# Second part of a feed-forward block as seven block products, with the sums of its weights made in the attention stages

## The chip, the core and the metric

The kernel runs on one core of a Trainium2 chip, in one launch. The metric is the device time of that launch in microseconds (us), here the median of several runs. Five engines work side by side, each through its own list of instructions and strictly in that list's order: TensorE (PE, matrix products, with PEld for the loads of its stationary operand), VectorE (DVE), ScalarE (ACT), GpSimd (POOL) and SyncE (SP). In this kernel SP issues nearly all DMAs, so a DMA that waits on SP holds back all DMAs that stand behind it there. An instruction waits by semaphores for the data, or for the buffer, that another engine hands over. The matrix products write to PSUM, of which this stage holds eight buffers of 128x512; everything else lies in SBUF, 128 partitions wide.

## The reference

One layer of a streaming-encoder block on 1024 tokens of width 1024, in float32: a token-mixing stage with two recurrent branches and an output projection `w_out`, a cross-attention into 256 memory tokens with the weights `xa_wq`, `xa_wk`, `xa_wv`, `xa_wo`, and a gated feed-forward block with a hidden width of 2816. The change concerns the last line before the final norm:

```python
h = h + (gate_a * y_a + gate_b * y_b) @ w_out[l]
...
u = rmsnorm(h, norm_xa_g[l])
...
h = h + o @ xa_wo[l]

u = rmsnorm(h, norm_ffn_g[l])
h = h + (jax.nn.silu(u @ ffn_w1[l]) * (u @ ffn_w3[l])) @ ffn_w2[l]
return rmsnorm(h, norm_final_g)
```

## The kernel before

**Products.** Every float32 operand is split into a high part (a copy rounded to the type fp32r, made by ACT) and a low part (the operand less the high part, made by POOL or DVE). `mm3` (L297 to L301) then adds up three products: high by high (L299), high by low (L300), low by high (L301). So each block product costs three matmuls, and each operand one ACT and one POOL or DVE instruction of 128x512 (`split`, L276 to L285).

**Stages near the end.** After the mixing stage come, in this order, the keys and values of the memory, `add_project` with `w_out` over all 1024 tokens (tile `pw`, four column blocks c of 256, 8 loads of tokens `tok`), the query projection and attention, `add_project` with `xa_wo` for one half of the tokens and then for the other, the feed-forward's first part (tile `P`), and its second part (tile `acc`). In `add_project` a column block takes four weight loads of 256 KB. Its products collect in PSUM and DVE adds them to the tokens (L1724); three PSUM buffers serve them.

**First part.** For each of 11 pairs f of hidden blocks, `products` makes seven block products per weight matrix (14 with both, 12 matmuls each) and from their sums four gated blocks of hidden values, which go to the DRAM array `hid_d` as [128 hidden x 512 tokens].

**Second part.** It is computed once per half h of the tokens and per half c of the output's columns. For each of these four, 22 hidden blocks are multiplied with four token tiles: 4 x 22 x 4 x 3 = 1056 matmuls of 128x512. The hidden blocks are loaded back and split once per half (ACT L2046, POOL L2047); 14 of the 22 lie in a ring of buffers (`th`, `tl`), the other 8 in the tiles `ah`, `al`. The blocks of `w2` are loaded and split 22 times for each of the four (`operand`, ACT L281, POOL L285), with seven buffers each for the parts `wh` and `wl`. The last three hidden blocks of each of the four are worked token tile by token tile, so that the four sums end one after another (`ILAST`).

**What sets the order.** The code issues instructions per block; a scheduler with its own estimates of durations puts them in each engine's list, SP's included. So loads and splits stand earlier or later in a list than the code says; the lists are shown below where it matters.

Of the kernel before, what the change touches and what calls it, by code (L numbers as in the profile page):

```python
# [17 lines left out]
P = 128  # L18
D = 1024
# [164 lines left out]
def tile_trunk(ctx, tc, x, mem, norm_mix_g, w_in, rw_mu, rw_w0, rw_w2, rw_a0, rw_a2, rw_g2,  # L184
# [1454 lines left out]
    early_d = scratch("early_d", [2, HK, P, HALF])  # L1639
    ssq = const.tile([P, 4, 4], F32, name="ssq")  # L1640
# [5 lines left out]
    def attention_block(xctx):  # L1646
# [27 lines left out]
        Kh = kp.tile([P, KT, NM], F32R, name="Kh")  # L1674
        Kl = kp.tile([P, KT, NM], F32R, name="Kl")
        Vh = vp.tile([P, NMT, D], F32R, name="Vh")
        Vl = vp.tile([P, NMT, D], F32R, name="Vl")
# [28 lines left out]
        def add_project(a, w, src, halves, ss=None, beside=iter(())):  # L1706
# [3 lines left out]
            for c in range(D // W):  # L1710
                ww = load_w(w, c * W)
                for i2 in range(2 * halves.start, 2 * halves.stop):
# [15 lines left out]
                    if c > 1 or c == 1 and i2 % 2:  # L1728
                        next(beside, None)
# [33 lines left out]
        hs = add_project(yT, w_out, x[0], range(NHALF))  # L1763
# [79 lines left out]
        for _ in prev:  # L1843
            pass

        for h in range(NHALF):
            hs = add_project(oT, xa_wo, h1d, range(h, h + 1), *((ssq, early_blocks(hs, *fa)) if h else ()))
# [23 lines left out]
    hd = scratch("hid_d", [FT, NHALF, P, HALF])  # L1871
    def raw(src, k, c, kn, cn):
# [20 lines left out]

    def blocks():

        return [[fp.tile([P, HALF], F32, tag=t, name=f"h{t}", bufs=4 if t == "s" else 2) for t in ts] for ts in (("u2", "u3"), ("c", "s"))
                for _ in range(2)]
# [47 lines left out]
    def gated(n, C, s, f, t):  # L1945

        if n == 0:
            s = fp.tile([P, HALF], F32, tag="s", name="s", bufs=4)
            nc.scalar.activation(s, C, AF.Sigmoid)
        nc.vector.tensor_tensor(s, C, s, op=ALU.mult)  # L1950
        if n:
            nc.sync.dma_start(out=hd[f, t], in_=s)
        return s

# [17 lines left out]
    def early_products(f, T1, T4):  # L1972

        for name, T, b in (("P5", T1, "S1"), ("P4", T4, "B22")):
            for n in range(2):
                t = kept[f, name, n] = fp.tile([P, HALF], F32, tag="kept", name=name, bufs=8)
                nc.scalar.activation(t, product(name, T[n], B[b]), AF.Copy)

    def products(f, A):
# [6 lines left out]
        for n in range(2):  # L1986
# [3 lines left out]
            s = gated(n, C, s, f, 1)  # L1990
        for a11, a12, a21, a22 in A:
# [38 lines left out]
    for f in range(HF):  # L2030
        products(f, weights(f))

    fg = fp.tile([P, D], F32, name="fg", bufs=1)
    nc.sync.dma_start(out=fg, in_=norm_final_g.partition_broadcast(P))
    order = [f + e for f in range(HF) for e in (0, HF)]
    ILAST = 3
    for h in range(NHALF):
        a = act(act1)
        hid = []
        for n, f in enumerate(order):  # L2040
            if n >= FT - KT:
                hh, hl = (t[:, n - FT + KT, :] for t in a)
            else:
                hh, hl = (ring.tile([P, HALF], F32R, tag=t, name=t) for t in ("th", "tl"))
# [3 lines left out]
            hid.append((hh, hl))  # L2048
        hs = blocks()
        for i in range(4):  # L2050
            for c in range(2):
                nc.sync.dma_start(out=hs[i][c], in_=h2d[(4 * h + i) * P:(4 * h + i + 1) * P, c * HALF:(c + 1) * HALF])
        ss = sp.tile([P, 4, 8], F32, tag="ssf", name="ssf")
        for c in range(2):
            cs = slice(c * HALF, (c + 1) * HALF)
            acc = [psum("acc") for _ in range(4)]
            w2 = []
            for n, f in enumerate(order):
                w2.append(operand(raw(ffn_w2, f, c * HALF, 1, HALF), "2"))
                if n < FT - ILAST:  # L2060
                    steps = [(i, n) for i in range(4)]
                elif n == FT - 1:
                    steps = [(i, g) for i in range(4) for g in range(FT - ILAST, FT)]
                else:
                    steps = []
                for i, g in steps:
                    ts_ = slice(i * P, (i + 1) * P)
                    mm3(acc[i], hid[g][0][:, ts_], hid[g][1][:, ts_], w2[g][0][:, 0, :], w2[g][1][:, 0, :],
                        g == 0, g == FT - 1)

            sums = []

            def finish(i):

                r = ss[:, 3, i:i + 1]
                o1, o2 = hs[i]
                rows = slice((4 * h + i) * P, (4 * h + i + 1) * P)
                nc.scalar.activation(o1, o1, AF.Copy, scale=r)
                nc.sync.dma_start(out=out[rows, 0:HALF], in_=o1)
                ins = nc.vector.scalar_tensor_tensor(o2, o2, r, fg[:, HALF:D], op0=ALU.mult, op1=ALU.mult).ins  # L2080
                behind(ins, sums[-1])
                nc.sync.dma_start(out=out[rows, HALF:D], in_=o2)

            for i in range(4):
                o = hs[i][c]
                r = [ss[:, n, i:i + 1] for n in range(4)]
                sums.append(nc.vector.tensor_tensor(o, acc[i], o, op=ALU.add).ins.name)  # L2087
# [37 lines left out]
```

## Time and profile before

| | |
|---|---|
| time, median of 3 runs | 2396.96 us (2396.28 to 2398.84) |
| the profiled execution's own time | 2398.55 us |
| its span in the trace | 2396.8 us |
| PE busy | 2335.8 us, 97% |
| DVE, ACT, POOL busy | 1411.2, 1128.3, 1228.8 us |
| mean granted clock of PE | 0.993 |
| second part: first and last matmul start | 2139.3 and 2389.4 us |

A matmul's record is longer than the time from one start to the next, since matmuls overlap; what a stretch of matmuls costs is read from the starts. An instruction's idle time before it and the engine that ended it stand in brackets in the rows of the timeline.

### The profile page before, as it was taken

The page shows a single profiled execution, that of the slowest core. Times are in us where ns is not written, and L with a number is a line of the kernel's source. Part 1 is how long each engine was busy: PE and PEld are TensorE (multiplying, and loading weights), DVE is VectorE, ACT ScalarE, POOL GpSimd, SP SyncE. Part 2 cuts the span into 40 slices and gives each one's busy share as a digit, 9 for nine tenths or more (in the row PEclk, how much of TensorE's full clock was granted, in tenths as well). Part 3 has the DMA queues.
Part 4 walks back from the last instruction along what each step waited for, and adds up shares of the span by engine and source line. Part 5 has one row for each costly group of instructions (what it writes and reads, how often), then busy time and mean ns, then how long its engine had stood idle before and what let it go on. Part 6 is the DMA issues. An engine that isn't in the chain of part 4 may idle for free. (4 is left out here: it accounts for less than half of the span.)

```text
span 2396.8 us, 48780 instructions
## 1 busy us (share of the span) xinstructions
PE 2335.8 (97%) x19258; PEld 1934.3 (81%) x19258; DVE 1411.2 (59%) x2288; ACT 1128.3 (47%) x2249; POOL 1228.8 (51%) x1268
## 2 busy tenths in 40 slices
PE   7999999999999999999998999999999999999998
PEld 5777777778887878888887998889778888877887
DVE  5887874667777667767754525444687565640101
ACT  6545454646566656555663415444433333343332
POOL 3554545555466555665664511112565444477673
PEclk9999999999999999999999999999999999999999
DMA  5444445333344343434244823133723223265441
GB/s 168 122 127 121 123 117 161 74 101 85 92 109 110 82 129 105 123 89 126 56 140 152 300 69 117 53 120 132 259 80 101 84 75 93 71 199 172 158 161 57
DMA packets 386001, 288.46 MB, mean 120 GB/s; under 512 B 106171, under 2 KB 329517, under 8 KB 385773
## 3 DMA queue, kind: packets, MB, share of 16 engines
q1 hardware_dynamic: 383341, 279.58, 39.6%
q0 software_dynamic: 1344, 4.72, 0.5%
q8 instruction: 152, 2.49, 0.4%
q10 hardware_dynamic: 1088, 1.05, 0.1%
q14 instruction: 76, 0.62, 0.1%
HBM read 208.73 MB, written 76.02 MB: 119 GB/s over the span
## 5 line engine op out<-in xcount | busy, mean ns | idle before, releaser
L102 PE MATMUL pproj<-uh,whi 128*128 128x512 f32 x768 | 320.0, 417 | 1.1 <-DVE q L102 1.1
L102 PE MATMUL pproj<-uh,wlo 128*128 128x512 f32 x768 | 300.9, 392 | 2.8 <-POOL wlo L102 2.1
L102 PE MATMUL pproj<-ul,whi 128*128 128x512 f32 x768 | 301.2, 392 | 0.0
L285 POOL TENSOR_TENSOR wl<-wraw,wh 128x512 fp32r<-128x512 f32 x154 | 202.1, 1323 | 133.2 <-ACT wh L281 131.6
L285 POOL TENSOR_TENSOR wlo<-wraw,whi 128x512 fp32r<-128x512 f32 (+1 forms) x86 | 117.9, 1374 | 288.6 <-ACT whi L281 280.7
L102 POOL TENSOR_TENSOR wlo<-wraw,whi 128x512 fp32r<-128x512 f32 x96 | 129.0, 1355 | 118.8 <-ACT whi L102 103.8
L281 ACT ACTIVATE whi<-wraw 128x512 fp32r<-128x512 f32 (+1 forms) x166 | 101.0, 617 | 173.1 <-PE pw L301 62.0
L299 PE MATMUL pproj<-uh,whi 128*128 128x512 f32 (+1 forms) x432 | 179.5, 416 | 0.9 <-ACT whi L281 0.6
L281 ACT ACTIVATE wh<-wraw 128x512 fp32r<-128x512 f32 x154 | 94.3, 627 | 182.2 <-PE P L300 74.5
L301 PE MATMUL pproj<-uh,wlo 128*128 128x512 f32 (+1 forms) x432 | 171.4, 397 | 1.5 <-POOL wlo L285 1.5
L102 PEld LDWEIGHTS pproj<-uh,whi 128*128 128x128 f32 x768 | 144.4, 188 | 34.3 <-DVE q L102 2.4
L300 PE MATMUL pproj<-ul,whi 128*128 128x512 f32 (+1 forms) x432 | 170.7, 395 | 0.0
L102 PEld LDWEIGHTS pproj<-ul,whi 128*128 128x128 f32 x768 | 144.3, 188 | 32.0
L102 PEld LDWEIGHTS pproj<-uh,wlo 128*128 128x128 f32 x768 | 144.9, 189 | 28.1 <-POOL wlo L102 2.5
L285 POOL TENSOR_TENSOR wlT<-wraw,whT 128x512 fp32r<-128x512 f32 x70 | 96.6, 1386 | 96.2 <-ACT whT L281 92.5
L299 PE MATMUL pw<-whi,ah 128*128 128x256 f32 x512 | 144.6, 282 | 0.0
L300 PE MATMUL pw<-wlo,ah 128*128 128x256 f32 x512 | 144.6, 282 | 0.0
L301 PE MATMUL pw<-whi,al 128*128 128x256 f32 x512 | 144.3, 282 | 0.0
L2087 DVE TENSOR_TENSOR hu<-acc,hu 128x512 f32<-128x512 f32 x8 | 5.5, 692 | 200.0 <-PE acc L301 200.0
L285 DVE TENSOR_TENSOR wlo<-wraw,whi 128x512 fp32r<-128x512 f32 x80 | 73.7, 922 | 83.4 <-ACT whi L281 83.1
L102 ACT ACT_TABLE_LOAD x90 | 115.5, 1283 | 13.5 <-DVE m L102 6.4
L299 PEld LDWEIGHTS pproj<-uh,whi 128*128 128x128 f32 (+1 forms) x432 | 81.6, 189 | 25.4 <-issue 6.2
(457 smaller groups left out, 6656.2 us busy)
## 6 DMA issues: line engine op xcount, KB each, us to landing
wraw<-in_ffn_w_dram SPq DMA_DIRECT2D x192, 256.0 KB
wraw<-in_w_in_dram SPq DMA_DIRECT2D x148, 256.0 KB
hid_d<-s SPq DMA_DIRECT2D x44, 256.0 KB
tok<-in_x_dram SPq DMA_DIRECT2D x16, 512.0 KB
ar_d<-AR SPq DMA_DIRECT2D x32, 256.0 KB
bk_d<-BK SPq DMA_DIRECT2D x16, 512.0 KB
AR<-ar_d SPq DMA_DIRECT2D x64, 128.0 KB
BK<-bk_d SPq DMA_DIRECT2D x16, 512.0 KB
```

The lines of the kernel that those rows point to most:

```text
L102: r = getattr(self.engine, op)(*a, **kw)
L281: nc.scalar.activation(hi, src, AF.Copy)
L285: e.tensor_tensor(lo, src, hi.bitcast(F32), op=ALU.subtract)
L299: nc.tensor.matmul(ps, ah, bh, start=first, stop=False)
L300: nc.tensor.matmul(ps, ah, bl, start=False, stop=False)
L301: nc.tensor.matmul(ps, al, bh, start=False, stop=last)
L2087: sums.append(nc.vector.tensor_tensor(o, acc[i], o, op=ALU.add).ins.name)
```

## The change

The second part takes seven block products in place of eight. The hidden values X (two halves of tokens by two halves of the hidden width) and W = `w2` (two halves of the hidden width by two halves of columns) are taken as 2 x 2 blocks, and four sums of blocks of each side, with seven products of them, give the four result blocks by additions.

- **Sums of the weights** (`w2_sums`). For each of 11 pairs of row blocks: two loads of 512 KB, two DVE and two POOL subtractions of 128x512 (L1717 to L1720), and one store of 1 MB to the array `wsum_d` (L1721). Seven of the pairs are done while `add_project` works on `w_out`, in the tiles of the pool `act2`; four while it works on `xa_wo` for the first half of the tokens, in the tiles that held the keys and values.
- **Sums of the hidden values** (`hidden_sums`). For each of 11 pairs, in the first part: two DVE and two POOL instructions of 128x512 (L2010 to L2013), and four stores to `hsum_d`. One of the four stores to `hid_d` goes. The gated blocks stay in a ring of 14 buffers (`kept`) until then.
- **The second part.** 7 blocks x 11 items x 4 token tiles x 3 = 924 matmuls. Every item loads one hidden block or sum and one block of `w2` or sum (77 of each). The low part of the hidden side is made by DVE (L2200) where POOL made it; all hidden operands lie in the ring of 20. The code splits four items ahead of the product and loads eight ahead.
- **Results.** The residual tokens lie in `act1` (tile `hres`), loaded by eight DMAs of 512 KB. Products that serve several result blocks are first added up in the tiles `Uw`, `Vw` (`p1`, `p5`, `p6`, `p7`) and added to `hres` by `more` (L2149).

The diff, cut to its core:

```diff
+        def w2_sums(fs, places):
...
+            def sums(f, y):
+                y11, y12, y21, y22 = (y[:, n, :] for n in range(4))
+                nc.vector.tensor_tensor(y11, y12, y11, op=ALU.subtract)
+                nc.gpsimd.tensor_tensor(y12, y22, y12, op=ALU.subtract)
+                nc.gpsimd.tensor_tensor(y22, y22, y11, op=ALU.subtract)
+                nc.vector.tensor_tensor(y21, y22, y21, op=ALU.subtract)
+                nc.sync.dma_start(out=wsd[f], in_=y)
...
-        hs = add_project(yT, w_out, x[0], range(NHALF))
+        hs = add_project(yT, w_out, x[0], range(NHALF), every=True, beside=w2_sums(
+            w2f, [None, None] + [in_act2(tag, n) for tag in ("ah", "al", "ah") for n in range(2)] + [in_act2("al", 0)]))
...
+    def hidden_sums(f):
+        x11, x21, x12, x22 = (hid.pop(k) for k in ((f, 0), (f, 1), (f + HF, 0), (f + HF, 1)))
+        tt(x22, x21, x22, op=ALU.add)
+        nc.gpsimd.tensor_tensor(x21, x11, x21, op=ALU.subtract)
+        tt(x11, x22, x11, op=ALU.subtract)
+        nc.gpsimd.tensor_tensor(x12, x12, x11, op=ALU.subtract)
+        for n, t in enumerate((x22, x11, x21, x12)):
+            nc.sync.dma_start(out=hsd[n, f], in_=t)
...
-            nc.sync.dma_start(out=hl.bitcast(F32), in_=hd[f, h])
-            nc.scalar.activation(hh, hl.bitcast(F32), AF.Copy)
-            nc.gpsimd.tensor_tensor(hl, hl.bitcast(F32), hh.bitcast(F32), op=ALU.subtract)
...
+    ILAST, LOOK, LOADS = 3, 4, 8
+    blocks = ((lambda f: hd[f, 0], w2(0, 0), p1),
+              (lambda f: hd[f + HF, 0], w2(1, 0), lambda i, acc: add(0, i, 0, acc, ALU.add, True)),
+              (lambda f: hsd[1, f], wsum(3), p6),
+              (lambda f: hsd[0, f], wsum(0), p5),
+              (lambda f: hsd[3, f], w2(1, 1), lambda i, acc: add(0, i, 1, acc, ALU.add, False)),
+              (lambda f: hsd[2, f], wsum(1), p7),
+              (lambda f: hd[f + HF, 1], wsum(2), lambda i, acc: add(1, i, 0, acc, ALU.subtract, False)))
...
+    def split_item(b, f):
+        hl, y = loaded.pop((b, f))
+        hh = ring.tile([P, HALF], F32R, tag="th", name="th")
+        nc.scalar.activation(hh, hl.bitcast(F32), AF.Copy)
+        tt(hl, hl.bitcast(F32), hh.bitcast(F32), op=ALU.subtract)
+        ops[b, f] = (hh, hl, *operand(y, "2"))
```

What the change makes of the engines' lists is shown at three places. The first is SP's list where `add_project` starts on `w_out`; `y` are the tiles of the weight sums, `tok` the tokens. Before:

```order
L1759 DMA yraw<-y_d 128x512 x12
L1667 DMA wraw<-in_w_out_dram 128x2x256 x10
L334 DMA tok<-in_x_dram 128x1024 x8
L1667 DMA wraw<-in_w_out_dram 128x2x256 x6
L1667 DMA wraw<-in_xa_wq_dram 128x2x256 x10
L1767 DMA h_d<-tok 128x1024 x6
```

And now, from behind the first block's four weight loads, which still stand first:

```order
L1713 DMA y_16881<-in_ffn_w_dram 128x1024 x3
L334 DMA tok<-in_x_dram 128x1024 x8
L1713 DMA y_16881<-in_ffn_w_dram 128x1024
L1668 DMA wraw<-in_w_out_dram 128x2x256 x4
L1713 DMA y_17016<-in_ffn_w_dram 128x1024 x2
L1721 DMA wsum_d<-y_16881 128x2048
L1713 DMA y_17016<-in_ffn_w_dram 128x1024 x2
L1721 DMA wsum_d<-y_16881 128x2048
L1721 DMA wsum_d<-y_17016 128x2048
L1713 DMA y_17133<-in_ffn_w_dram 128x1024 x4
L1721 DMA wsum_d<-y_17016 128x2048
L1668 DMA wraw<-in_w_out_dram 128x2x256 x4
```

The second column block's four now stand behind eight 512 KB loads of tokens and four of sums; the third block's four stand behind four stores of finished sums.

The second place is DVE's list over the same stretch; `al` are low parts of the tokens' operands, `wlo` of the weights, and `tok<-pw` adds a product from PSUM to the tokens. Before:

```order
L285 TENSOR_TENSOR wlo<-wraw,whi 128x512 x2
L285 TENSOR_TENSOR al<-yraw,ah 128x512
L1702 TENSOR_TENSOR Vl<-pvv,Vh 128x2x256
L285 TENSOR_TENSOR al<-yraw,ah 128x512 x3
L285 TENSOR_TENSOR wlo<-wraw,whi 128x512
L1724 TENSOR_TENSOR tok<-pw,tok 128x256 x6
L285 TENSOR_TENSOR wlo<-wraw,whi 128x512
L1724 TENSOR_TENSOR tok<-pw,tok 128x256 x2
```

And now:

```order
L285 TENSOR_TENSOR wlo<-wraw,whi 128x512 x2
L1717 TENSOR_TENSOR y_16881<-y_16881 128x512
L285 TENSOR_TENSOR al<-yraw,ah 128x512
L1703 TENSOR_TENSOR Vl<-pvv,Vh 128x2x256
L285 TENSOR_TENSOR al<-yraw,ah 128x512
L1720 TENSOR_TENSOR y_16881<-y_16881 128x512
L285 TENSOR_TENSOR al<-yraw,ah 128x512 x2
L1717 TENSOR_TENSOR y_16881<-y_16881 128x512
L1758 TENSOR_TENSOR tok<-pw,tok 128x256 x6
L1720 TENSOR_TENSOR y_16881<-y_16881 128x512
L285 TENSOR_TENSOR wlo<-wraw,whi 128x512 x2
L1717 TENSOR_TENSOR y_17016<-y_17016 128x512
```

Two sums now stand among the low parts, and both weight splits of the second column block stand behind the last sum (L1720) of the second pair, which itself reads what two instructions of POOL write. In the lists of the changed kernel the line numbers are its own.

The third place is the border between the feed-forward's two parts. First POOL's list, where `wl` is the low part of a weight and `tl` that of a hidden block. Before:

```order
L285 TENSOR_TENSOR wl_23781<-wraw,wh_23780 128x512
L2047 TENSOR_TENSOR tl<-tl,th 128x512 x3
L285 TENSOR_TENSOR wl_23802<-wraw,wh_23801 128x512
L2047 TENSOR_TENSOR tl<-tl,th 128x512
L285 TENSOR_TENSOR wl_23943<-wraw,wh_23942 128x512
L2047 TENSOR_TENSOR tl<-tl,th 128x512 x2
L285 TENSOR_TENSOR wl_23961<-wraw,wh_23960 128x512
L2047 TENSOR_TENSOR tl<-tl,th 128x512 x2
L285 TENSOR_TENSOR wl_23979<-wraw,wh_23978 128x512
L285 TENSOR_TENSOR wl_23997<-wraw,wh_23996 128x512
```

And now:

```order
L285 TENSOR_TENSOR wl_24127<-wraw,wh_24126 128x512
L285 TENSOR_TENSOR wl_24150<-wraw,wh_24149 128x512
L2011 TENSOR_TENSOR s<-s 128x512
L2013 TENSOR_TENSOR s<-s 128x512
L285 TENSOR_TENSOR wl_24173<-wraw,wh_24172 128x512
L285 TENSOR_TENSOR wl_24196<-wraw,wh_24195 128x512
L285 TENSOR_TENSOR wl_24219<-wraw,wh_24218 128x512
L285 TENSOR_TENSOR wl_24242<-wraw,wh_24241 128x512
```

The hidden side's `tl` is gone from POOL (it stands on DVE), and the last pair's two sums (`s`) stand between the splits of weights. On SP, at the same border, `hid_d` is stored from `s` and loaded to `tl`, `h_d` are the residual tokens. Before:

```order
L2045 DMA tl<-hid_d 128x512 x2
L1875 DMA wraw<-in_ffn_w_dram 128x512 x2
L2052 DMA hc<-h_d 128x512
L1875 DMA wraw<-in_ffn_w_dram 128x512
L1952 DMA hid_d<-s 128x512
L2052 DMA hc<-h_d 128x512
L1875 DMA wraw<-in_ffn_w_dram 128x512
L2052 DMA hu_23920<-h_d 128x512
L2045 DMA al<-hid_d 128x512 x2
L1952 DMA hid_d<-s 128x512
L2045 DMA al<-hid_d 128x512 x6
```

And now:

```order
L1998 DMA hid_d<-s 128x512
L1924 DMA wraw<-in_ffn_w_dram 128x512
L2106 DMA hres<-h_d 128x1024 x2
L1998 DMA hid_d<-s 128x512
L2101 DMA fg<-in_norm_final_g_dram 128x512 x2
L2106 DMA hres<-h_d 128x1024
L1998 DMA hid_d<-s 128x512
L2106 DMA hres<-h_d 128x1024 x2
L2015 DMA hsum_d<-s 128x512 x4
L2106 DMA hres<-h_d 128x1024 x3
L2193 DMA tl<-hid_d 128x512 x5
L1924 DMA wraw<-in_ffn_w_dram 128x512
```

All eight loads of residual tokens and the last four stores of sums now stand ahead of the loads of the eleventh and later hidden blocks (`tl` x5).

## Rows read from the trace of the kernel before

**Rows 1.** The page: span, busy time by engine, GB/s in 40 slices.
```profile
span 2396.8 us, 48780 instructions
...
PE 2335.8 (97%) x19258; PEld 1934.3 (81%) x19258; DVE 1411.2 (59%) x2288; ACT 1128.3 (47%) x2249; POOL 1228.8 (51%) x1268
...
GB/s 168 122 127 121 123 117 161 74 101 85 92 109 110 82 129 105 123 89 126 56 140 152 300 69 117 53 120 132 259 80 101 84 75 93 71 199 172 158 161 57
```

**Rows 2.** Windows by stage: us, busy us by engine, PEclk, DMA share, GB/s.
```profile
1360.00:1454.00 94.00, 93.95 (x784) 93.72 (x782) 32.23 (x52) 23.30 (x41) 21.04 (x15) 1.00 0.39 136
...
1604.00:1670.00 66.00, 65.95 (x558) 65.22 (x557) 24.83 (x41) 23.28 (x46) 15.78 (x12) 1.00 0.41 136
1760.00:2100.00 340.00, 340.00 (x1491) 279.53 (x1490) 226.66 (x290) 109.79 (x181) 166.60 (x125) 1.00 0.28 86
2139.00:2390.00 251.00, 244.06 (x1059) 198.23 (x1057) 32.49 (x49) 80.63 (x150) 161.17 (x131) 1.00 0.43 141
```

**Rows 3.** Tile acc: count, ns min/median/max, first and last start.
```profile
L299 PE MATMUL acc<-wh,th x224: 387/390/502, 2139.3 to 2366.7; 128*128 128x512 f32 x112
...
L301 PE MATMUL acc<-wh,al x128: 390/393/405, 2186.5 to 2389.4; 128*128 128x512 f32 x128
```

**Rows 4.** Timeline of PE in the second part, operands in the ring: start, us, instruction.
```profile
2214.76 0.39 PE L300 MATMUL acc<-wl,th 128*128 128x512 f32 x1
...
2224.96 0.39 PE L300 MATMUL acc<-wl,th 128*128 128x512 f32 x1
```

**Rows 5.** The same at its end, operands in `ah`, `al`.
```profile
2382.71 0.39 PE L299 MATMUL acc<-wh,ah 128*128 128x512 f32 x1
...
2389.45 0.40 PE L301 MATMUL acc<-wh,al 128*128 128x512 f32 x1
```

**Rows 6.** Waits of PE from 2090 us on: total, times, longest.
```profile
PE acc L299 <- DVE C L2010: 3.3, 1, 3.3
PE acc L300 <- POOL wl L285: 3.3, 3, 1.9
```

**Rows 7.** Groups by line in the second part: count, busy us, mean ns, idle before.
```profile
L285 POOL TENSOR_TENSOR wl<-wraw,wh 128x512 fp32r<-128x512 f32 x86 | 110.5, 1300 | 47.9 <-ACT wh L281 46.4 <-issue 1.4
...
L281 ACT ACTIVATE wh<-wraw 128x512 fp32r<-128x512 f32 x84 | 51.1, 625 | 90.5 <-PE acc L301 71.9 <-DMA wraw<-in_ffn_w_dram 8.5 <-POOL wl L285 3.9
```

**Rows 8.** Groups of DVE in the first part.
```profile
L1950 DVE TENSOR_TENSOR s<-U,s 128x512 f32<-128x512 f32 x39 | 42.4, 1088 | 6.2 <-ACT s L1949 4.2 <-DMA wraw<-in_ffn_w_dram 1.4
...
L2003 DVE TENSOR_TENSOR U<-P,U 128x512 f32<-128x512 f32 x20 | 13.7, 683 | 0.0
```

**Rows 9.** Timeline at the border of the two parts, DVE and POOL.
```profile
2137.13 6.47 DVE L1950 TENSOR_TENSOR s<-C,s 128x512 f32<-128x512 f32 x1 [10.19 <-ACT s L1949]
...
2138.04 2.55 POOL L2047 TENSOR_TENSOR tl<-tl,th 128x512 fp32r<-128x512 f32 x2
...
2140.52 2.52 POOL L285 TENSOR_TENSOR wl<-wraw,wh 128x512 fp32r<-128x512 f32 x2
```

**Rows 10.** Windows: the stretch that loads tokens, and one of the second part.
```profile
1355.00:1380.00 25.00, 25.00 (x211) 25.00 (x210) 13.53 (x15) 8.71 (x16) 10.76 (x7) 1.00 0.91 316
...
2260.00:2300.00 40.00, 40.00 (x177) 32.99 (x176) 8.74 (x12) 18.68 (x35) 30.41 (x27) 1.00 0.72 241
```

**Rows 11.** Timeline of ACT: the splits of the weights of `w_out`.
```profile
1357.66 2.78 ACT L281 ACTIVATE whi<-wraw 128x512 fp32r<-128x512 f32 x4 [2.08 <-DMA wraw<-in_w_out_dram]
...
1381.88 2.75 ACT L281 ACTIVATE whi<-wraw 128x512 fp32r<-128x512 f32 x4 [15.03 <-issue]
1404.92 2.75 ACT L281 ACTIVATE whi<-wraw 128x512 fp32r<-128x512 f32 x4 [20.30 <-PE pw L301]
```

**Rows 12.** Timeline of POOL: low parts of the second half's tokens.
```profile
1363.29 6.63 POOL L285 TENSOR_TENSOR al<-yraw,ah 128x512 fp32r<-128x512 f32 x4 [0.21 <-ACT ah L281]
```

**Rows 13.** Windows at two waits of PE before `w_out`.
```profile
1345.00:1350.00 5.00, 2.06 (x12) 1.81 (x12) 4.43 (x4) 4.14 (x8) 5.00 (x4) 0.80 0.85 304
1350.00:1355.00 5.00, 5.00 (x26) 5.00 (x25) 3.44 (x4) 1.65 (x3) 3.20 (x3) 0.51 0.51 153
```

More of the change, by code (lines that the diff above doesn't have):

```diff
@@ L1704, in attention_block, with load, add_project @@
             nc.sync.dma_start(out=t[:, 0:KEYS, :].bitcast(F32), in_=kd[n])
-        def add_project(a, w, src, halves, ss=None, beside=iter(())):
+        def w2_sums(fs, places):
+            def load(f, y):
+                for r in range(2):
+                    rows = slice((f + r * HF) * P, (f + r * HF + 1) * P)
+                    nc.sync.dma_start(out=y[:, 2 * r:2 * r + 2, :].rearrange("p c t -> p (c t)"), in_=ffn_w2[0, rows, :])
+            def sums(f, y):
[5 more added lines that the diff above has]
+                nc.sync.dma_start(out=wsd[f], in_=y)
+            loaded = []
+            for place in places:
+                if place:
+                    y = place()
+                    f = next(fs)
+                    load(f, y)
+                    loaded.append((f, y))
+                    if len(loaded) < 3:
+                        yield
+                        continue
+                if loaded:
+                    sums(*loaded.pop(0))
+                yield
+            for l in loaded:
+                sums(*l)
+                yield
+        def add_project(a, w, src, halves, ss=None, beside=iter(()), every=False):
             hs = []
@@ L1844, in attention_block @@
             pass
+        in_kv = [lambda p=p, t=t: p.tile([P, 4, HALF], F32, tag=t, name="y2")
+                 for p, t in ((kp, "Kh"), (kp, "Kl"), (vp, "Vh"), (vp, "Vl"))]
         for h in range(NHALF):
-            hs = add_project(oT, xa_wo, h1d, range(h, h + 1), *((ssq, early_blocks(hs, *fa)) if h else ()))
+            hs = add_project(oT, xa_wo, h1d, range(h, h + 1), *((ssq, early_blocks(hs, *fa)) if h else ()),
+                             **({} if h else dict(beside=w2_sums(w2f, in_kv), every=True)))
             for i in range(4):
@@ new lines, in tile_trunk, with load_item @@
+    items = [(b, f) for b in range(len(blocks)) for f in range(HF)]
+    loaded, ops, acc = {}, {}, None
+    def load_item(b, f):
+        t = ring.tile([P, HALF], F32R, tag="tl", name="tl")
+        nc.sync.dma_start(out=t.bitcast(F32), in_=blocks[b][0](f))
+        loaded[b, f] = t, blocks[b][1](f)
+    def split_item(b, f):
[4 more added lines that the diff above has]
+        ops[b, f] = (hh, hl, *operand(y, "2"))
@@ new lines, in tile_trunk @@
+    for item in items[:LOADS]:
+        load_item(*item)
+    for item in items[:LOOK]:
+        split_item(*item)
+    for n, (b, f) in enumerate(items):
+        if n + LOADS < len(items):
+            load_item(*items[n + LOADS])
+        if n + LOOK < len(items):
+            split_item(*items[n + LOOK])
+        if f == 0:
+            acc = [psum("acc") for _ in range(4)]
+        if f < HF - ILAST:
+            steps = [(i, f) for i in range(4)]
+        elif f == HF - 1:
+            steps = [(i, g) for i in range(4) for g in range(HF - ILAST, HF)]
+        else:
+            steps = []
+        for i, g in steps:
+            hh, hl, yh, yl = ops[b, g]
+            ts_ = slice(i * P, (i + 1) * P)
+            mm3(acc[i], hh[:, ts_], hl[:, ts_], yh[:, 0, :], yl[:, 0, :], g == 0, g == HF - 1)
+        if later:
+            more(*later.pop(0))
+        if f == HF - 1:
+            for i in range(4):
+                blocks[b][2](i, acc[i])
```

156 lines of the change are left out of this document (90 added, 66 removed).

## The prediction

> **What bounds the kernel now.** I read the page first: PE is busy for 2335.8 of 2396.8 us [rows 1], far above every other engine, so a gain has to come from PE's list, and work on DVE, ACT, POOL or the DMA engines counts only where PE waits for it. Then the windows by stage [rows 2]: PE does not idle while `add_project` works on `w_out` (93.95 of 94 us) and on `xa_wo` (65.95 of 66), nor in the feed-forward's first part (340 of 340); in the second part it is busy 244.06 of 251 us. There DVE works 32 us, ACT 81 and POOL 161 of the 251. Then the second part alone: matmuls start from 2139.3 to 2389.4 [rows 3], so with the last one's 0.40 us [rows 5] it takes 250.5 us, and 7 us from its end to that of the span. The waits of PE in it add up to 6.6 us [rows 6].
>
> **The second part's products.** Before there are 1056 matmuls, 672 with operands in the ring (three rows of 224) and 384 with operands in `ah`, `al` (three of 128) [rows 3]. The pitch in the ring is 10.20 us over 45 starts, 0.2267 us [rows 4]; in `ah`, `al` it is 6.74 us over 29, 0.2324 us [rows 5]. 672 x 0.2267 = 152.3, 384 x 0.2324 = 89.2, with the waits 248.1; the missing 2.4 us are slower starts behind each wait. Now there are 924, all in the ring: 924 x 0.2267 = 209.5 us. If PE finds its operands ready, the part takes 209.5 in place of 250.5: 41 us less. 30.2 of that are the 132 products that go (at the mean pitch before, 0.2287), 1.8 come from the faster pitch of the others, 9.0 from the waits and the slow starts behind them; the last only if no new waits come.
>
> Are the operands ready? An item keeps PE for 12 x 0.2267 = 2.72 us and asks POOL for one low part (1.30 us), ACT for two high parts (2 x 0.625) [rows 7] and DVE for one low part, 0.69 us where nothing disturbs it (the 683 ns of an addition from PSUM is the nearest undisturbed row, 1.09 the mean of a DVE multiplication of two SBUF operands beside POOL) [rows 8]. POOL is filled by 1.30 of 2.72, ACT by 1.25, DVE by 0.7 to 1.1, to which the blocks' ends add some 36 DVE additions in all, 8 POOL multiplications and ACT's 8 squares and 4 copies. No engine comes near the 2.72. With seven buffers for `wh`, `wl` the split of an item's weight may begin when the item seven before it is done, over 16 us ahead of its use; behind the last three items of a block, which end together, that shrinks to about 11 us. So I put the steady state at no wait.
>
> The transfers: 154 blocks of 256 KB are 40.4 MB, the residual tokens and the output 4.2 MB each, 48.8 MB in 209.5 us or 233 GB/s. In a window of the second part before, 241 GB/s ran at a DMA share of 0.72 with PE busy for the whole 40 us, and 316 GB/s at 0.91 while tokens were loaded [rows 10]. I take it as hidden.
>
> **The border of the two parts.** Before, one DVE multiplication took 6.47 us while POOL ran without a gap (five low parts on end) [rows 9]; what stood behind it on DVE, the additions that free PSUM, came late, and PE waited 3.3 us for one [rows 6]. The `tl` of that run go to DVE, and POOL's remaining splits come at PE's pace, so this wait goes. Next late there is the eleventh hidden block's load: on SP it stands behind eight loads of residual tokens (4.2 MB) and four stores of sums that wait for the last pair's sums, some 7 us behind the last product of the first part. The loads of residual tokens start when the tiles are free, 5.4 us ahead of the border (24 matmuls of the last two products); 1.0 MB of stores and the rest of the 4.2 MB then take some 14 us at 0.316 MB/us [rows 10], and the block is split by 17 us. PE needs it after eight items and a little, at 22 us. I charge 1 us for this border, 0 to 6.
>
> Here a rule of the Trainium skill bears on the change. The row says that DVE's multiplication got through only when POOL's run ended: 6.47 us [rows 9], five times one POOL instruction. The skill's page "SBUF — State Buffer", section "Who interferes with whom", says that a DVE instruction with two SBUF inputs and a GpSimd instruction that reads SBUF exclude each other, and the second to issue blocks until the first has finished: by it a DVE low part would take at most 1.30 + 0.69 = 1.99 us, so an item still fits in 2.72 and the sum holds. By the row DVE waits for a whole run of POOL; that is the second rival below.
>
> **The sums of the hidden values** add two DVE and two POOL instructions to each of 11 pairs, a pair taking 14 x 12 x 0.2267 = 38.1 us. DVE is busy for 226.7 of 340 us there, POOL for 166.6 [rows 2]; 2 x 1.09 and 2 x 1.30 lift both by 6% or 7% of a pair. Stores rise by three of 256 KB a pair, 21 GB/s on top of 86. Both hide beside PE; the stores hold back four weight loads on SP by some 6 us, and those are split some 15 us behind their issue. 0.5 us, bounds 0 and 4.
>
> **The sums of the weights at `w_out`.** DVE works 32, POOL 21 of 94 us, the DMA engines 39% [rows 2]. Seven pairs add 14 x 0.69 to 14 x 1.09 us on DVE, 14 x 1.30 on POOL, and 14.7 MB: room enough on average. The place where it is not free is the start. Before, ten weight loads and the tokens (6.8 MB) were in by 1380, at a mean of 316 GB/s [rows 10]; now 1.0 MB of weights, 2.1 of sums, 4.2 of tokens and then the second block's 1.0 are 8.4 MB, which is 5 us later, 1385, the first of the block's four near 1382. Before, that block's last splits stood at 1381.88, as the first block let go of its buffers, and PE came to it some 2 us later, 1383.6 (a block takes 23.0 us, from 1381.88 to 1404.92) [rows 11]. Now the first split takes 0.6 and 1.3 us from 1382 on, and POOL and DVE are both behind the second pair's sums, which wait for the load behind the tokens. So PE starts the block 1 to 3 us late. The four low parts on POOL took 1363.29 to 1369.92 [rows 12], and are needed half a block, 11.5 us, behind the stage's start near 1360.5, from 1372 on; two sums among them make that close, and cost 0 to 1. The third block's loads stand behind four 1 MB stores and the sums they wait for; they go out near 1395 and land by 1406, needed at 1407 to 1409: 0 to 2. I take 2.5 us, between 0.5 and 6.
>
> How high can this go? At two waits just ahead of this stage PE was busy for 2.06 of 5 us, and the granted clock was 0.80 and 0.51 in these and the next 5 us [rows 13], two fifths of the one stretch and nearly all of the other at 1.2 in place of 2.4 GHz. That costs (0.20 + 0.49) x 5 = 3.4 us at most besides the wait. The upper bound for the stage becomes 9.5 us.
>
> **The sums at `xa_wo`.** One sum stands on DVE ahead of the last head's low part, and the loads wait for the tiles of keys and values. PE idles 0.05 of 66 us now [rows 2]; the weights of three and a half column blocks are loaded ahead of it. 0.5 us, bounds 0 and 3.
>
> **The sum.** -41.0 + 1 + 0.5 + 2.5 + 0.5 = -36.5 us. The profiled execution took 2398.55, so it would take 2362.0; the median of the runs is 1.6 us below it, and 2396.96 - 36.5 = 2360.5. I forecast 2361 us. With the lower bounds of all four costs the gain is 40.5 and the time 2356.5; with the upper ones (6, 4, 9.5, 3) it is 18.5 and 2378.5. As these will not all fall together, the case's own range is 2354 to 2370.
>
> **Rivals.**
> - *SP's list becomes the wait at `w_out`.* Stores stand on it until sums are done, the sums stand on DVE behind additions that wait for PE, and the third and fourth column block's weights come behind them. For it: the order, and that the loads come to within 2 us of their need. Against it: DMA engines idle for 61% of the stage. Two column blocks each 4 us late and the clock lost at both (2 x 3.4) make 15 where I put 2.5: 2373 us, from 2367 to 2380. Chance 0.14.
> - *DVE starves beside POOL in the second part.* It now makes 77 low parts of two SBUF operands; behind each block's last three items POOL has three or four splits on end, and DVE's additions from PSUM wait behind a low part. A wait of 3.3 us [rows 6] at each of seven blocks is 23 us: 2384 us, from 2375 to 2393. Against it: eight PSUM buffers, four per block, so that a block's additions have some 30 us. Chance 0.10.
> - *The DMA engines become the bound, and it is slower than before.* The four full slices of the second part moved 158 to 199 GB/s [rows 1]. If two streams of 2 KB pieces in and stores out hold no more than 172, 48.8 MB take 284 us in place of 250.5, with the other 4.5 us 2435. It decides below 48.8 MB in 246 us, 198 GB/s. Against it: 241 GB/s at a share of 0.72 [rows 10]; before, the rate was what was asked for. Chance 0.07, with 2400 to 2435.
> - *The change leaves PE as long.* The lists hold 924 matmuls of `acc` and the pitch is that of the same tile shapes, so I give it 0.02 (2393 to 2397).
>
> The main case has 0.67. Range for 8 in 10: 2353 to 2383, which leaves out half of the second rival and the last two. What a measurement of this kernel tells from no change is about 0.2%, 4.8 us: faster by more 0.90, within 0.03, slower by more 0.07.
>
> **What would show it.** Right: `acc` with 924 matmuls at 0.2267 us, first to last start 209 to 212 us, no PE wait over 1 us in it; the 6.47 us multiplication gone; the second column block of `w_out` 1 to 3 us late behind a weight split, PE busy 88 to 93 of that stage's 94 us; first part as before. Wrong: waits of `acc` for `tl` on DVE or for a DMA, a DMA share near 1 over the second part, a granted clock below 1 in it, or a `w_out` stage over 100 us. If the gain falls under 25 us, the step that failed is one of the four "hidden" above, and the stage with PE's waits names it.

## The result and the profile after

The changed kernel takes 2384.06 us (median of 4 runs, 2383.37 to 2384.93) against 2396.62 (4 runs, 2395.86 to 2398.84): ratio 0.9946, 95% interval 0.9929 to 0.9963. It is faster by 12.6 us, where 36 were forecast, and lies 1 us outside the range. None of the named rivals happened, though one of them ("DVE starves beside POOL") had this very time.

The page after, against [rows 1]: PE has 132 instructions and 22.7 us less, and DVE 135 us more.

```profile
span 2381.7 us, 48869 instructions
...
PE 2313.1 (97%) x19126; PEld 1914.4 (80%) x19126; DVE 1546.4 (65%) x2441; ACT 1133.3 (48%) x2271; POOL 1243.1 (52%) x1257
```

The tile `acc` after, against [rows 3]: 924 matmuls (three of 308), all in the ring, from 2151.9 to 2373.7. With 0.4 us for the last one the second part takes 222.2 us; 250.5 before, 209.5 predicted. The longest one in these two rows takes 793 ns, twice the median; it starts at 2334.32, in a window with a granted clock of 0.66 (below).

```profile
L299 PE MATMUL acc<-wh,th x308: 387/389/793, 2151.9 to 2373.2; 128*128 128x512 f32 x154
...
L301 PE MATMUL acc<-wh,tl x308: 388/389/628, 2152.3 to 2373.7; 128*128 128x512 f32 x154
```

Windows after by stage, with the columns of [rows 2]; PEclk is the clock that PE was granted, as a share of 2.4 GHz. PE is no longer full at `w_out` and `xa_wo`, and it is not full in the second part, at a DMA share of 0.56 with DVE, ACT and POOL each busy for about half of it. No resource is used up.

```profile
1360.00:1460.00 100.00, 95.42 (x777) 94.45 (x776) 44.12 (x66) 24.16 (x43) 40.13 (x29) 0.99 0.76 274
1604.00:1670.00 66.00, 62.82 (x499) 61.35 (x498) 30.40 (x52) 20.67 (x41) 23.05 (x17) 0.95 0.79 287
...
2151.00:2374.00 223.00, 215.59 (x929) 176.07 (x927) 116.13 (x142) 93.10 (x175) 119.48 (x88) 0.98 0.56 193
```

Where the time went, in us, from the first and last starts of the tiles `pproj`, `pq`, `P` and `acc` in both profiles. The profiled pair is 15.1 us apart in span, the medians 12.6.

| stretch | before | after | difference | predicted |
|---|---|---|---|---|
| start to the last `pproj` | 1314.0 | 1315.0 | +1.0 | 0 |
| to the last `pq` (with `w_out`) | 280.0 | 284.0 | +4.0 | +2.5 |
| to the first `P` (with `xa_wo`) | 104.5 | 111.3 | +6.8 | +0.5 |
| to the first `acc` (first part, border) | 440.8 | 441.6 | +0.8 | +1.5 |
| second part | 250.5 | 222.2 | -28.3 | -41.0 |
| tail | 7.0 | 7.6 | +0.6 | 0 |

So three stretches miss: the second part by 12.7 us, `xa_wo` by 6.3, `w_out` by 1.5. The waits of PE name the places (from 1290 us on):

```profile
PE acc L299 <- ACT wh L281: 6.0, 2, 4.8
PE pw L300 <- POOL wlo L285: 4.5, 3, 1.9
...
PE pw L300 <- DVE wlo L285: 2.2, 2, 1.3
```

**The second part.** PE waits 1.23 and 0.84 us near 2297, and 4.78 and 0.56 near 2335. Around them (same columns) the granted clock is 0.91 and 0.66, so slow matmuls come on top of the waits:

```profile
2290.00:2300.00 10.00, 7.93 (x29) 5.69 (x28) 6.49 (x7) 4.26 (x8) 4.84 (x4) 0.91 0.45 157
...
2330.00:2340.00 10.00, 5.12 (x13) 3.76 (x14) 5.08 (x7) 5.01 (x10) 4.34 (x4) 0.66 0.62 218
```

Three timelines around the first wait, ACT, POOL, then SP (start, us, instruction, idle before). ACT splits the last block's hidden blocks (`tl<-hid_d`, 12 items ahead of the weight beside them) in front of the `wh` that PE needs at once:

```profile
2295.37 0.63 ACT L2199 ACTIVATE th<-tl 128x512 fp32r<-128x512 f32 x1 [2.63 <-DMA tl<-hid_d]
2295.91 0.61 ACT L281 ACTIVATE wh<-wraw 128x512 fp32r<-128x512 f32 x1
2298.29 0.63 ACT L2199 ACTIVATE th<-tl 128x512 fp32r<-128x512 f32 x1 [1.77 <-DMA tl<-hid_d]
2298.83 0.62 ACT L281 ACTIVATE wh<-wraw 128x512 fp32r<-128x512 f32 x1
```

```profile
2290.31 1.35 POOL L285 TENSOR_TENSOR wl<-wraw,wh 128x512 fp32r<-128x512 f32 x1 [3.48 <-DMA wraw<-wsum_d]
...
2296.60 1.26 POOL L285 TENSOR_TENSOR wl<-wraw,wh 128x512 fp32r<-128x512 f32 x1 [2.04 <-ACT wh L281]
```

```profile
2291.68 0.32 SPq L2175 DMA_DIRECT2D wraw<-wsum_d  x1
2292.11 0.37 SPq L2193 DMA_DIRECT2D tl<-hid_d  x1
...
2297.89 0.32 SPq L2175 DMA_DIRECT2D wraw<-wsum_d  x1
2298.31 0.37 SPq L2193 DMA_DIRECT2D tl<-hid_d  x1
```

Read them as one loop. POOL's low part ends at 2291.66 and frees one of ten `wraw` buffers. SP issues the weight load that waited for it (2291.68) and behind it the hidden block (2292.11). ACT waits for that block until 2295.37, then makes `wh` at 2295.91; POOL's low part of it ends at 2297.86, SP issues at 2297.89. By the lists of the three engines `wh` of item n stands behind `th` of item n+12, whose load stands behind the weight load of n+8, which waits for `wl` of n-2. Two such rounds run side by side (the other one passes SP at 2294.59 and 2300.82), so one round of 6.2 us serves 2 items, 3.1 us each, where PE takes 2.72. From 2292.12 to 2309.04 five `wh` took 16.9 us, 3.4 each. The lead of seven `wh` buffers is eaten up, and PE waits.

The longer wait, near 2333, has the same order on ACT, but what holds the hidden block is another entry of SP's list: from 2313.46 to 2325.72 SP issues the eight stores of the first half's output, with one hidden block's load between them, and the next such load goes out at 2328.33. ACT sits idle for it with the `wh` that PE needs right behind it, at 2333.66:

```profile
2325.72 0.33 SPq L2145 DMA_DIRECT2D out_dram<-hres  x1
...
2328.33 0.38 SPq L2193 DMA_DIRECT2D tl<-hid_d  x1
```

```profile
2333.12 0.63 ACT L2199 ACTIVATE th<-tl 128x512 fp32r<-128x512 f32 x1 [11.72 <-DMA tl<-hid_d]
```

**`xa_wo`.** POOL and DVE after (columns of a timeline). ACT had all four `whi` ready at 1632.7, but POOL's two low parts stand behind lines 1718 and 1719 of a sum, and DVE's behind its line 1720:

```profile
1631.58 1.30 POOL L1718 TENSOR_TENSOR y<-y 128x512 f32<-128x512 f32 x1 [2.07 <-DVE y L1717]
1632.96 1.27 POOL L1719 TENSOR_TENSOR y<-y 128x512 f32<-128x512 f32 x1
1634.19 2.94 POOL L285 TENSOR_TENSOR wlo<-wraw,whi 128x512 fp32r<-128x512 f32 x2
```

```profile
1630.82 0.68 DVE L1717 TENSOR_TENSOR y<-y 128x512 f32<-128x512 f32 x1
1634.26 1.73 DVE L1720 TENSOR_TENSOR y<-y 128x512 f32<-128x512 f32 x1 [2.76 <-POOL y L1719]
1635.92 1.76 DVE L285 TENSOR_TENSOR wlo<-wraw,whi 128x512 fp32r<-128x512 f32 x1
```

The chain DVE, POOL, POOL, DVE lasts from 1630.82 to 1635.99. PE waits 1.9 and 0.9 us for low parts here. The clock makes most of the rest of the 6.8 us, 0.80 and 0.86 in the two windows, (0.20 + 0.14) x 10 = 3.4 us at most:

```profile
1630.00:1640.00 10.00, 7.15 (x47) 6.65 (x46) 6.18 (x9) 2.53 (x4) 5.47 (x4) 0.80 0.61 207
1640.00:1650.00 10.00, 10.00 (x79) 10.00 (x78) 2.34 (x5) 2.53 (x4) 2.10 (x2) 0.86 1.02 371
```

**`w_out`.** PE waits for low parts at the second column block and for DVE's addition from PSUM at the third. The first two have the forecast cause: POOL's low parts stand behind a sum that waited 10.41 us for its load. At the third DVE's addition stands behind L1720, which waited for POOL:

```profile
1385.81 0.38 PE L300 MATMUL pw<-wlo,ah 128*128 128x256 f32 x1 [1.63 <-POOL wlo L285]
1388.04 0.39 PE L300 MATMUL pw<-wlo,ah 128*128 128x256 f32 x1 [1.26 <-DVE wlo L285]
1412.00 0.39 PE L299 MATMUL pw<-whi,ah 128*128 128x256 f32 x1 [1.26 <-DVE tok L1758]
```

```profile
1381.88 1.29 POOL L1718 TENSOR_TENSOR y<-y 128x512 f32<-128x512 f32 x1 [10.41 <-DMA y<-in_ffn_w_dram]
...
1384.50 2.94 POOL L285 TENSOR_TENSOR wlo<-wraw,whi 128x512 fp32r<-128x512 f32 x2
```

```profile
1409.50 1.77 DVE L1720 TENSOR_TENSOR y<-y 128x512 f32<-128x512 f32 x1 [2.78 <-POOL y L1719]
1411.20 0.74 DVE L1758 TENSOR_TENSOR tok<-pw,tok 128x256 f32<-128x256 f32 x2
```

### The profile page after: what moved, and what is told of

It reads as the page before. It is cut to its first block, busy times and chain, and to the rows that moved or that the text cites. A ratio compares the mean times of both kernels' runs of the same rounds, so it can differ in the third digit from the quotient of the medians.

```text
span 2381.7 us, 48869 instructions
## 1 busy us (share of the span) xinstructions
PE 2313.1 (97%) x19126; PEld 1914.4 (80%) x19126; DVE 1546.4 (65%) x2441; ACT 1133.3 (48%) x2271; POOL 1243.1 (52%) x1257
## 5 line engine op out<-in xcount | busy, mean ns | idle before, releaser
L285 POOL TENSOR_TENSOR wlT<-wraw,whT 128x512 fp32r<-128x512 f32 x70 | 103.5, 1496 | 69.3 <-ACT whT L281 64.9
L2200 DVE TENSOR_TENSOR tl<-tl,th 128x512 fp32r<-128x512 f32 x77 | 75.9, 1013 | 79.6 <-ACT th L2199 78.2
L299 PE MATMUL acc<-wh,th 128*128 128x512 f32 x308 | 121.4, 394 | 6.0 <-ACT wh L281 6.0
L300 PE MATMUL acc<-wl,th 128*128 128x512 f32 x308 | 121.7, 395 | 1.4 <-POOL wl L285 1.4
L301 PE MATMUL acc<-wh,tl 128*128 128x512 f32 x308 | 121.2, 394 | 0.0
```

The source lines that it names most:

```text
L285: e.tensor_tensor(lo, src, hi.bitcast(F32), op=ALU.subtract)
L299: nc.tensor.matmul(ps, ah, bh, start=first, stop=False)
L300: nc.tensor.matmul(ps, ah, bl, start=False, stop=False)
L301: nc.tensor.matmul(ps, al, bh, start=False, stop=last)
L2200: tt(hl, hl.bitcast(F32), hh.bitcast(F32), op=ALU.subtract)
```

## The experiments

All times below are medians. "Second part", "`w_out`" and "`xa_wo`" are the stretches of the table, each read from the one profiled run of its kernel. The kernel before had 2397.1 to 2397.5 us beside these runs. Each experiment changes the changed kernel; its edit is shown shortened.

**1. Output stores behind the last load (e1_out_late).**

```
-        nc.sync.dma_start(out=out[rows, ...], in_=o1)      # in finish(), half 0; o2 alike
+        stores.append((out[rows, ...], o1))                # issued behind the last load_item
```

> Changed: the eight stores of the first half's output are issued behind the last load of a hidden block on SP's list, instead of ahead of the loads for the last block. The changed kernel's second part lasts 222 us (first start of acc to its end), PE waits in it are 1.2 and 0.8 us near 2296 and 4.8 us near 2333, each with slow clock behind it. Theory A (a loop through three lists: ACT's split of a hidden block 12 items ahead stands in front of the split of the weight needed next; that hidden block's load stands on SP behind a weight load, whose buffer is freed only by POOL's low part, which waits for ACT): the wait near 2296 stays, the one near 2333 shrinks to under 2.5 us and the part takes 216 to 219. Theory B (only the output stores hold SP's list): the wait near 2333 goes with its slow clock, the one near 2296 stays, since no store is issued by then: 215 to 217. Theory C (low parts on DVE and POOL slow each other): nothing moves, 221 to 223. In time 2384 becomes 2377 to 2381 by A, 2376 to 2378 by B, 2384 by C.

Measured: 2380.04 us, second part 216.0 (in the fastest of the four runs, 2376.34). Theory C falls. The part alone fits theories A and B, the median time A. The waits speak for A: they did not go but spread, six of them up to 2330, the longest 1.0 us:

```profile
PE acc L300 <- POOL wl L285: 3.0, 4, 1.0
PE acc L299 <- ACT wh L281: 1.3, 2, 1.0
```

**2. Hidden blocks and weights split in step (e2_wh_first).**

```
+        if whs: behind(th_ins, whs[-1])     # order on ACT: th(n) after wh(n-1)
```

> Changed: on ACT the split of a hidden block is tied behind the high part of the weight one item earlier, so the two go in step and a hidden block is no longer split some 12 items ahead; the output stores stay where they are. Theory A (loop through ACT, POOL and SP): both waits, near 2296 and near 2333, go, since weights are split up to seven items ahead and 10 + 7 items stand between SP and PE; the part takes 210 to 213 us in place of 222, the time is 2372 to 2376. Theory B (the stores hold SP): the wait near 2333 stays at 4 to 5 us with the slow clock, 217 to 220, 2379 to 2382. Theory C (DVE and POOL slow each other): 221 to 223, 2384.

Measured: 2370.75 us, second part 209.6, no wait of PE in it. On SP seven loads stand one or two rows later than before and the stores stay in front of the same loads, but for one. Theory A holds by its mechanism, with the part 0.4 us and the time 1.3 us below its range; theories B and C fall.

**3. The four subtractions of a weight sum on DVE (e3_sums_dve).**

```
-                nc.gpsimd.tensor_tensor(y12, ...); nc.gpsimd.tensor_tensor(y22, ...)
+                nc.vector.tensor_tensor(y12, ...); nc.vector.tensor_tensor(y22, ...)
```

> Changed: all four subtractions of a weight sum at w_out and xa_wo run on DVE, instead of DVE, POOL, POOL, DVE in a chain; second part untouched. The changed kernel loses 6.8 us at xa_wo (from the last pq to the first P, against the kernel before) and 3.8 at w_out (last pproj to first pq). Theory D (the chain of four between two engines stands for 5.5 us in front of weight splits on both lists): xa_wo loses 0 to 2 us, with granted clock 1 there; w_out loses 1 to 4, since its second block's weights are loaded late as well; time 2376 to 2380. Theory E (loads and stores of the sums on SP make the weights late): both losses stay, 6 to 7 and 3 to 5, time 2383 to 2385.

Measured: 2375.56 us, `w_out` 280.0 and `xa_wo` 104.5, both as long as before; second part 221.8. SP's list is the same row by row. Theory D holds; theory E falls, at `w_out` too, where D had still allowed 1 to 4 us for late loads (PE still waits 0.8 us for one low part there). Windows at `xa_wo`: PE full, DVE takes the sums (9.38 us in 10), and the DMA share of 0.95 and 1.01 costs nothing.

```profile
1620.00:1630.00 10.00, 10.00 (x91) 10.00 (x90) 9.38 (x16) 1.72 (x3) 2.24 (x2) 1.00 0.95 392
1630.00:1640.00 10.00, 10.00 (x91) 10.00 (x90) 3.75 (x6) 1.73 (x3) 2.45 (x2) 1.00 1.01 333
```

**4. No subtractions, all transfers (e4_no_sums).** The lines 1716 to 1720 go.

> Left out: the four subtractions of each weight sum at w_out and xa_wo; the weights are loaded and stored as they are, so the second part multiplies by other numbers at the same cost. All transfers stay as in the changed kernel. Theory D (the subtractions stand in front of the weight splits): xa_wo loses 0 to 1 us, w_out keeps 1 to 3 us from late loads; time 2375 to 2379. Theory E (loads and stores make the weights late): xa_wo still loses 5 to 7, w_out 3 to 5; time 2382 to 2385.

Measured: 2373.1 us (2368.78 to 2378.28), `w_out` 280.1, `xa_wo` 106.0. Theory E falls again. Theory D holds at `xa_wo`, where 1.5 us are lost in place of 0 to 1, but the time is 2 us below its range, and its loss of 1 to 3 us at `w_out` is not there. (The untouched second part took 224.9 us in the profiled run, the slowest of the four.)

**5. Experiments 2 and 3 together (e5_both).**

> Changed: the order on ACT (each hidden block's split behind the high part of the weight one item earlier) and all four subtractions of a weight sum on DVE, together. If the two losses are independent (theory), the gains add: the second part takes 210 us, xa_wo and w_out lose nothing against the kernel before, and the time is 2370.75 - 8.6 = 2362, from 2359 to 2365. Rival: sums that end earlier or later shift SP's loads so that a wait comes back in the first or second part; then 2366 to 2372.

Measured: 2360.58 us (2359.48 to 2362.51), ratio to before 0.9848 (0.9832 to 0.9864). The gains add, and the rival falls; `xa_wo` took 106.0, `w_out` 280.1. It beats both kernels, and is the version to keep. Its `acc` rows: no matmul over 389 ns, first to last start 209.2 us.

```profile
L299 PE MATMUL acc<-wh,th x308: 389/389/389, 2143.5 to 2352.2; 128*128 128x512 f32 x154
...
L301 PE MATMUL acc<-wh,tl x308: 388/389/389, 2143.9 to 2352.7; 128*128 128x512 f32 x154
```

**6. Weights loaded from POOL's queue (e6_w_queue).**

```
-            nc.sync.dma_start(out=t[:, 0, :], in_=wsd[f, :, n, :])     # and ffn_w2 alike
+            nc.gpsimd.dma_start(out=t[:, 0, :], in_=wsd[f, :, n, :])
```

> Changed: in the second part the weights (and their sums) are loaded from POOL's queue instead of SP's; SP issues hidden blocks and output stores alone, and ACT's order stays as in the changed kernel. Theory A (the loop closes on SP, where a hidden block's load stands behind a weight load that waits for a buffer): the wait near 2296 goes (under 0.5 us before 2310), the one near 2333 stays at 2 to 5 us, since the output stores still hold the hidden blocks' loads that ACT splits ahead of the next weight; the part takes 215 to 219. Rival (ACT's order alone costs it, whatever the queue): both waits stay, 221 to 223. Rival F (a load issued by POOL costs POOL so much that low parts come late): over 224.

Measured: 2384.81 us, second part 221.2: by its time the rival's number, a miss. The waits say otherwise: from 2200 us on PE waits nowhere, neither near 2296 nor near 2333, though the stores still stand on SP and ACT's lead is still 12 items. What it lost lies at the part's start, where PE waits for two low parts and then for a hidden block, whose load SP issues only from 2174 us on, behind stores and token loads (granted clock 0.90 from 2150 to 2200):

```profile
2173.74 0.50 PE L300 MATMUL acc<-wl,th 128*128 128x512 f32 x1 [0.62 <-POOL wl L285]
2175.90 0.50 PE L300 MATMUL acc<-wl,th 128*128 128x512 f32 x1 [1.19 <-POOL wl L285]
2183.11 0.79 PE L299 MATMUL acc<-wh,th 128*128 128x512 f32 x1 [6.48 <-ACT th L2205]
```

So the loop needs SP's leg, and A's second half (the stores hold PE by themselves) fell. Also new, and not explained here: the end of the span is 10.9 us behind the last matmul in place of 7.6.

**7. The four subtractions on POOL (e7_sums_pool).** As 3, with `nc.gpsimd` for all four.

> Changed: all four subtractions of a weight sum at w_out and xa_wo run on POOL. Theory D (what stands in front of the weight splits costs the time, and a sum on POOL alone takes 4 x 1.29 = 5.2 us, as long as the chain of 5.5): xa_wo still loses 4 to 8 us, by waits for wlo on POOL alone and none for DVE; time 2381 to 2386. Rival (the hand-offs between the engines cost it, not the length of the work on POOL's list): 0 to 2 us, 2375 to 2378.

Measured: 2387.93 us (2385.00 to 2390.57), `xa_wo` 113.0, `w_out` 286.3. Theory D holds by its mechanism, 0.5 us beyond its range at `xa_wo` and 2 us in time: there is one wait, on POOL alone, longer than a sum, because two sums stood ahead of the low parts. The rival falls: without any hand-off the loss is larger. In experiment 3 two sums stood ahead of DVE's low parts just so, but DVE takes 0.69 us for a subtraction where POOL takes 1.29, and was done in time. Its waits at `xa_wo`:

```profile
PE pw L300 <- POOL wlo L285: 6.3, 1, 6.3
```

**8. Experiment 5 with late output stores (e8_all).**

> Changed: both edits of e5 and the late output stores of the first run. Theory A: once hidden blocks and weights are split in step, the stores on SP cost nothing, so this is as e5 within 2 us and the second part 209 to 211. Rival B (the stores still hold SP): 2 to 5 us faster than e5.

Measured: 2362.15 us (2360.61 to 2367.14), second part 209.6 as in 5. Rival B falls: with the loop gone the stores cost nothing.

**9 and 10. One item less lead on ACT, with late stores (e9_lead) and alone (e10_lead_only).**

```
+        if len(whs) >= 12: behind(th_ins, whs[-12])     # th(n) after wh(n-12)
```

A stretch of ACT's list, the splits numbered by item (1 to 77), in the changed kernel and in experiment 10:

```
changed kernel   th 43   th 44   wh 32   th 45   wh 33   th 46   wh 34
experiment 10    th 43   wh 32   th 44   wh 33   th 45   wh 34   th 46
```

In all, 22 hidden splits stand later, 20 of them by one row. POOL's list is the same; on SP one hidden block's load stands behind one more store.

> Changed: the late output stores of the first run, and on ACT a hidden block's split may stand at most 11 items ahead of the next weight's high part instead of 12; SP's order of loads is the same. Theory A in numbers: high part n waits behind the split of hidden block n+12, whose load stands on SP behind the weight load n+8, which waits for the buffer that low part n-2 frees; one round of this takes 6.2 us (low part's end 2291.66 to 2297.86) and serves 2 items, 3.1 us each where PE takes 2.72. With 11 a round serves 3 items, 2.07 us each, so the loop no longer sets the pace: no wait of PE over 0.3 us, second part 209.5 to 211 us in place of 216.0 in the first run, time 2373 to 2375. Rival G (what helped in the second run is that hidden and weight splits alternate, which spares DVE and POOL runs): one item changes next to nothing, 215 to 216.5, 2379 to 2381.

> Changed: only the lead on ACT, 11 items in place of 12; the output stores stand where the changed kernel has them. Theory A: the wait near 2296 goes; the stores still hold SP for some 13 us near 2313 to 2326, and 11 items of lead leave little behind them, so a wait near 2333 stays with 1 to 5 us: second part 212 to 217, time 2376 to 2380. Rival B' (the stores cost nothing unless the loop has used up the lead, as when the weights came from POOL's queue): 209.5 to 211, 2373 to 2375. Rival G (one item changes nothing): 221 to 223, 2384.

Measured: 2371.74 and 2370.92 us, second part 209.6 in both, no wait of PE; both times are 1 to 2 us below the ranges named. One item less lead on one list is worth 12.6 us of 222.2; G falls, and A's numbers for the loop hold. Alone it does as well as with late stores, so B' is right: in experiment 10 ACT still waits 10 us for a hidden block behind the stores, and PE stays full, because `wh` is ahead again.

```profile
2318.43 0.63 ACT L2200 ACTIVATE th<-tl 128x512 fp32r<-128x512 f32 x1 [10.06 <-DMA tl<-hid_d]
```

```profile
2310.00:2320.00 10.00, 10.00 (x46) 8.28 (x45) 4.19 (x4) 1.39 (x3) 2.68 (x3) 1.00 0.81 272
2320.00:2330.00 10.00, 10.00 (x46) 8.29 (x45) 9.08 (x13) 6.47 (x13) 8.08 (x6) 1.00 0.21 71
```

**All twelve profiles together.** The stretch up to the last `pproj`, which no edit touches, lasts 1313.4 to 1319.6 us, so whole times differ by some us that belong to no edit, and the stretches decide. With the chain of DVE and POOL (six kernels) `w_out` takes 283.9 to 285.7 us and `xa_wo` 110.2 to 111.4; with the subtractions on DVE or none (four) 280.0 to 280.7 and 104.5 to 106.2. With the loop and the stores as in the changed kernel (four) the second part takes 220.5 to 224.9 us; with 11 items of lead or fewer (five) 209.6 each time.

## Why the prediction was wrong, point by point

- **The products: right.** 924 x 0.2267 = 209.5 us was forecast, and 209.6 measured wherever the lists let PE run (experiments 2, 5, 8, 9, 10). The shorter product count and the faster pitch are both there.
- **"So I put the steady state at no wait": the step that failed, 12.7 us.** It compared each engine's work with 2.72 us per item and took the seven `wh` buffers as the only limit on the lead. The work was reckoned rightly, but it does not decide. What decides is the order of the lists: the scheduler let `th` run 12 items ahead although the code asks for four, and that lead closed a loop through ACT, SP's loads and POOL's freed buffers with 3.1 us an item. Used up like this, the lead was gone when the output stores held SP's list, and the second wait followed; with 11 items the same stores cost nothing. The lists are fixed before a run. The prediction read them at three places, and ACT's at none; from the lead in items, the ten `wraw` buffers and a load's 3 us the loop could have been worked out.
- **Transfers hidden: right.** 193 GB/s at a share of 0.56, where 233 were reckoned; the waits stand at 157 and 218 GB/s. What costs is not the rate but that a load's time lies inside the loop.
- **The border: right.** The 3.3 us wait [rows 6] and the 6.47 us multiplication [rows 9] are gone; PE waits nowhere between 2085 and 2165. With the hidden sums 0.8 us in place of 1.5. It was closer than reckoned: the eleventh hidden block was split at 2172.99, 21 us behind the border in place of 17, and PE came to it at its 103rd matmul, 2175.01. Experiment 6 shows what it costs to miss that, a wait of 6.48 us.
- **`w_out`, 2.5 us: right in size, the mechanism in part.** Measured 4.0, inside 0.5 to 9.5. The second column block was 2.9 us late behind low parts that stood behind a sum, as forecast. The third was 1.3 us late, but by an addition on DVE behind the chain and not by its loads. With the same list on SP and the chain gone (experiments 3, 4) nothing is lost, so the late loads alone, charged with most of the 2.5, cost next to nothing.
- **`xa_wo`, 0.5 us with 0 to 3: the second failed step, 6.8 us.** It looked at the one sum ahead of the last head and at loads. The sums themselves, handed back and forth in front of the weight splits on both lists, cost 2.8 us of waits, and the clock behind them most of the rest. The clock had been priced at `w_out` only.
- **The rivals.** SP's list at `w_out`: not seen. DVE starved beside POOL: its time of 2384 came true and its mechanism did not; in the best version DVE's `tl` take 1.34 us on average, longer than the 1.01 of the changed kernel, and PE never waits for them. So that time is a coincidence; a right number is no proof of a cause. The other two did not happen either: the DMA share is 0.56, and 924 matmuls ran at the forecast pitch.
- **The checks named for being wrong** pointed to the right places, waits of `acc` and a clock below 1, but not to the cause: the waits were for `wh` on ACT, and no check named `wh`. `xa_wo` is among them only as one of the terms called hidden.
- **The sum.** With the lists put right experiment 5 takes 2360.58 us, where 2361 were forecast. Its stretches lose 0.1 at `w_out`, 1.5 at `xa_wo`, 2.5 up to the first `acc` and 0.6 at the end, 4.7 in place of 4.5 but in other places, so that the agreement to half a microsecond is partly luck.

## What to carry to other kernels

Engines half idle and buffers deep enough don't make a pipeline: write down, from each engine's list, which instruction stands in front of the one that is due next, follow it through the load and the buffer it needs back to the engine it started from, and divide the round's time by the items it serves. A split that runs further ahead than its neighbour is no reserve if it stands in the same list. Before work is put into idle time, look on every list that it touches for the next instruction that is due, and count how long the work stands in front of it: here a sum of 2.8 us on DVE cost no more than no subtractions at all, one of 5.2 us on DVE and POOL in turns cost 6.8 us at `xa_wo`, and POOL alone, where a sum takes as long but two stood in front, cost 8.5.

## What the runs showed of the hardware

A wait can cost more than itself, and need not. At `xa_wo` 2.8 us of waits went with a loss of 6.8 us, the granted clock being 0.80 and 0.86 of 2.4 GHz in the windows with them and behind them. At `w_out` waits of 1.63, 1.26 and 1.26 us went with a loss of 4.0 us, and the granted clock in their windows, 1380 to 1390 and 1410 to 1420, was 1.00.

DVE beside POOL is uneven. In the changed kernel no `tl` took longer than 1.79 us; with weight loads issued by POOL one took 6.21, about as long as the multiplication of [rows 9].

```profile
L2200 DVE TENSOR_TENSOR tl<-tl,th x77: 677/693/1793, 2123.5 to 2337.4; 128x512 fp32r<-128x512 f32 x77
```

```profile
L2206 DVE TENSOR_TENSOR tl<-tl,th x77: 674/973/6211, 2122.7 to 2331.1; 128x512 fp32r<-128x512 f32 x77
```

The Trainium skill's page "SBUF — State Buffer", section "Who interferes with whom", says of a DVE instruction with two SBUF inputs beside a GpSimd instruction that reads SBUF that they contend: the one that issues first has the shared ports for its whole instruction and the other blocks. If that means a wait for one instruction of POOL, the first row agrees (under 1.30 + 0.69 us); the second does not, and the measurement decides.

A load issued by POOL takes 0.56 us of POOL, mostly 0.30 us behind the end of the low part ahead of it (experiment 6):

```profile
2270.54 1.28 POOL L285 TENSOR_TENSOR wl<-wraw,wh 128x512 fp32r<-128x512 f32 x1
2272.12 0.56 POOL L2181 DMA_DIRECT2D wraw<-wsum_d  x1 [0.30 <-POOL wl L285]
```
